# Preparation steps held on VectorE behind three more splits, and none ahead of a head's scores

## The chip, the cores and the metric

The kernel runs on one core of a Trainium2 chip. Its work goes through five engines, each with its own queue of instructions that it takes in order: TensorE (PE: matmuls and transposes), VectorE (DVE) and ScalarE (ACT) for elementwise work, GpSimd (POOL) and SyncE (SP), of which SP only starts transfers here and POOL starts some as well. An engine whose next instruction waits for something waits with everything behind it.

The metric is the device time of one launch in microseconds (us). Three runs of the kernel before gave 1018.87, 1021.4 and 1025.79 us, a median of 1021.4 us.

## The reference, cut to what matters

Two layers on `x` of 512 tokens by 1024 features, each `x = x + Mixer(RMSNorm(x))`: first gated linear attention (GLA), then a state-space mixer (S5), then a last RMSNorm. All is float32.

```python
# GLA: 4 heads, key size 128, value size 512; q, k, v, z, r are slices of h @ w_in
log_a = log_sigmoid(r @ w_gate_up + b_gate) / 16
b     = cumsum(log_a) within a chunk
att   = causal_mask((q * exp(b)) @ (k * exp(-b)).T)     # "scores"
o     = att @ v + (q * exp(b)) @ state_before_the_chunk  # state is carried from chunk to chunk
out   = (rms(o) * head_gain * silu(z)) @ w_out

# S5: 128 groups of 16 channels, 64 complex states each; u, z = split(h @ w_in)
lam_bar = exp(lam * dt);  b_bar = (lam_bar - 1) / lam * B
s_t   = lam_bar * s_(t-1) + b_bar @ u_t
y     = gelu(Re(C @ s) + d * u);  y = y * sigmoid(y @ w_glu + b_glu) * silu(z)
out   = y @ w_out
```

What S5 needs of powers of `lam_bar`, of `b_bar` and of `C` does not depend on `x`. The kernel builds these tables on the chip while the GLA layer runs. That is the "preparation" of the title.

## The kernel before, in words

**Arithmetic.** A float32 product is made of three matmuls on operands that are split in a high and a low part (`three`, L187 to L195): high by high, high by low, low by high. So every operand has to be split first: `split` (L155 to L162) writes the high part with ScalarE and the low part, source minus high, with VectorE; `split1` (L164 to L168) does both on VectorE.

**Weights.** They come in tiles of 128 x 1024 (512 KB), one load on SP's queue each (`wunit`, L173 to L184). Most are split by L158 (ScalarE) and L159 (VectorE). For `w_z`, `w_qk` and `w_v` of heads 1 to 3 (`dma=True`) the low part is made by a ScalarE copy and a GpSimd transfer that adds the source to it, so VectorE isn't needed there.

**The GLA layer** takes about the first 490 us, the S5 layer the rest. A head `h` of 1 to 3 goes so. The gate of the head (L422 to L446). The projections of q and k (`proj_qk`; VectorE takes them out of the PSUM banks at L460 and L461 and splits q at L159). Between these the output of the head before is transposed (`turn`: L399 on TensorE, L402 and a split on VectorE). Then the "weave", in which three things follow one another, one weight tile at a time: the projection of v (4 tiles), the product of the previous head's output with `w_out` (2 to 4 tiles), and the projection of z (4 tiles). Between the tiles the head's own attention is set in by a table of positions: `scores` (L484 a matmul, L486 a transpose of k, L488 the masked copy by VectorE, then splits), `state` (L502 to L506, splits at L170 and L171) and `mix`. The v tiles end in four PSUM banks `pd`, which VectorE and ScalarE empty at L161 and L162; the next tiles need these banks. The z tiles end in the same banks, emptied at L387 and L389, and the `w_out` tiles at L532.

**The preparation.** A plan of 43 steps lies ready: 17 F steps (tables from loaded constants, L1283 to L1301, and L1313; stores L1307 to L1309; then four loads for the next F step, among them `lpt` L1267, `s_bi` L1269 and `s_xc` L1272), 16 Z steps (L1323 on TensorE, L1327 on ScalarE, L1329 to L1333 on VectorE, a copy on SP that is called `gmd` here), 8 E steps (48 VectorE instructions on 128 x 512, L1251 to L1256, and transfers) and 2 G steps. A function `hook` is called once for each weight tile of the weave, and adds a rate to a counter; each time the counter passes one, a step is taken off the plan:

```python
pace[0] += RATES[phase[0]]      # phase is h - 1 for head h
while pace[0] >= 1: ...
    prep.step(mark, *st)
```

For heads 1 to 3, `hook` is also called `QZ[0]` times ahead of the head's weave, that is ahead of its scores. A head has 12 tiles in its weave, so before 14 calls of `hook`, at a rate of 0.84 or 0.88.

**What sets the order.** Tile, the layer that the kernel is written in, puts each engine's instructions in one fixed order when it builds the kernel. It may move instructions that do not depend on each other. A step of the preparation is held by `issue_after(mark[k])` for each of "pe", "act", "dve" and "sp": on each of these engines it may not stand ahead of the instruction last noted in `mark`. `mark["pe"]` is the last matmul of a `three`, `mark["sp"]` the last weight load, `mark["act"]` the last split of a weight tile on ScalarE; `mark["dve"]` is noted in `wunit` alone, and there only for the tiles that VectorE splits.

A part of the preparation that comes before the plan, called "small" (L985 to L1226), runs during head 0.

Of the kernel before, what the change touches and what calls it, by code (L numbers as in the profile page):

```python
# [19 lines left out]
MUL, ADD, SUB = ALU.mult, ALU.add, ALU.subtract  # L20

P = 128
# [37 lines left out]
USP = 50  # L60
SEQ0 = 'h0 u h2 u h4 u s h6 u x0 t x1 q0 q1 t'
GP = 4
RATES = [0.84, 0.84, 0.88, 0.94, 0.94]
LOWS = {'F': 30, 'Z': 30, 'E': 100, 'G': 0}
ETABS = [2, 3, 3, 3, 3, 3, 3, 3, 4, 4, 4, 4, 4, 4, 4, 7, 8]
POS = [[0, 0, 1, 2, 1, 2, 3, 1, 2, 3, 3], [0, 1, 1, 3, 4, 5, 6, 5, 5, 7, 9], [0, 1, 3, 4, 4, 5, 6, 5, 6, 8, 8], [1,
# [9 lines left out]
TORD = ['c0 c1 s0 c2 x0 s1 x1 c3 s2 x2 x3', 'c0 c1 c2 c3 x0 s0 s1 x1 s2 x2 x3', 'c0 c1 c2 c3 s0 x0 s1 s2 x1 x2 x3',  # L76
    'c0 c1 c2 c3 s0 s1 x0 x1 s2 x2 x3']
PACE = [2, 2, 2, 2, 2, 2, 3, 1, 2, 2, 2, 2, 2, 2, 2, 2, 2, 2, 1, 1, 1, 1]
QZ = [2, 3]
GPOS = [0, 0, 7]  # L80


def f(t):
    return t.bitcast(F32) if t.dtype == F32R else t
# [3 lines left out]
def trunk_kernel(  # L88
# [6 lines left out]
    V, A, G, S, PE = nc.vector, nc.scalar, nc.gpsimd, nc.sync, nc.tensor  # L95
# [58 lines left out]
    mark = {}  # L154
# [10 lines left out]
    def split1(dst_hi, dst_lo, src, scale=None):  # L165
        if scale is None:
            V.tensor_copy(out=dst_hi, in_=src)
            V.tensor_tensor(out=dst_lo, in0=src, in1=f(dst_hi), op=SUB)  # L168
        else:
            V.tensor_scalar(out=dst_hi, in0=src, scalar1=scale, scalar2=None, op0=MUL)  # L170
            V.scalar_tensor_tensor(out=dst_lo, in0=src, scalar=scale, in1=f(dst_hi), op0=MUL, op1=SUB)  # L171

    def wunit(src, nk, ncol, dma=False):  # L173
        raw = T_([P, nk, ncol], "wraw", WR)
# [150 lines left out]
    sm = prep.small(lam_re, lam_im, log_dt, s_d)  # L325
# [34 lines left out]
    def hook():  # L360
        pace[0] += RATES[phase[0]]
        while pace[0] >= 1:
# [29 lines left out]
    def turn(box, out_):  # L392
        oh, ol = out_

        def fn(tb):
            o2 = box[0][tb]
            pt = PT()
            for k in range(4):
                PE.transpose(pt[:, k * P:(k + 1) * P], o2[:, k * P:(k + 1) * P], ident)  # L399
            oh.append(q2(F32R))  # L400
            ol.append(q2(F32R))
            V.tensor_tensor(out=o2.rearrange("p (k c) -> p k c", k=4), in0=pt.rearrange("p (k c) -> p k c", k=4),  # L402
                            in1=hgp.unsqueeze(2).to_broadcast([P, 4, P]), op=MUL)
            split(oh[tb], ol[tb], o2)
        return fn

    rT = g4[:16, 1]
# [41 lines left out]
    def proj_qk(h, eq, ek):  # L449
        aq, ak = PO(), PO()  # L450
        for u in range(2):
            hi, lo = wunit(w_qk[h, u], 4, 256, dma=True)
            for m, acc in enumerate((aq, ak)):
                for k in range(4):
                    kb = 4 * u + k
                    three(acc, hi[:, k, m * P:(m + 1) * P], lo[:, k, m * P:(m + 1) * P],
                          hh[kb], hl[kb], kb == 0, kb == 7, True)
        q = eq
        k_ = ek
        V.scalar_tensor_tensor(out=q, in0=aq, scalar=float(P) ** -0.5, in1=eq, op0=MUL, op1=MUL)  # L460
        V.tensor_tensor(out=k_, in0=ak, in1=ek, op=MUL)  # L461
        qh = big(F32R)
        ql = big(F32R)
        split(qh, ql, q)
        return q, k_, qh, ql

    att_bufs = []
# [5 lines left out]
    class Attn:  # L473
# [6 lines left out]
        def scores(self, b):  # L480
            q, k_, qh, ql = self.qk
            cs = slice(b * P, (b + 1) * P)
            pa = PT()
            PE.matmul(pa[:, :P], lhsT=k_[:, cs], rhs=q[:, cs], start=True, stop=True)  # L484
            if b < NT - 1:
                PE.transpose(pa[:, P:2 * P], k_[:, cs], ident)  # L486
            at = att_bufs[b % 2]
            V.copy_predicated(out=at, mask=cmask, data=pa[:, :P])  # L488
            sm = self.sm[b] = big(F32R)
            if b < NT - 1:  # L490
                split(sm[:, 2 * P:3 * P], sm[:, 3 * P:], pa[:, P:2 * P])
            split1(sm[:, 0:P], sm[:, P:2 * P], at)

        def state(self, b):
            es, sm = self.es, self.sm[b]
# [922 lines left out]
```

## Time and profile before

| | |
|---|---|
| median of three runs | 1021.4 us |
| lowest and highest | 1018.87 and 1025.79 us |
| the profiled execution's own time | 1022.88 us |
| its span in the trace | 1021.1 us |
| mean granted TensorE clock | 0.946 of full speed |
| PE busy | 922.1 us, 90% of the span |
| VectorE busy | 716.5 us, 70% |
| ScalarE busy | 461.3 us, 45% |
| GpSimd busy | 138.3 us, 14% |

The trace is of one execution. A row of a timeline has the start, the duration, the engine, the line of the kernel, the operation, output and inputs by the program's names, their shape, and in brackets the time that the engine sat idle before it and what released it. An instruction's duration includes its latency; the next one of the same engine starts earlier than its end, so what a row of instructions takes is read from the distance of their starts. The granted clock of TensorE is given as a share of the full one: 1.00 is the higher of its two levels, 0.5 the lower.

### The profile page before, as it was taken

How to read it: one execution, taken by the hardware profiler on the slowest of the kernel's cores; microseconds unless marked ns; L12 is line 12 of the kernel's file. 1: busy time of each engine (PE TensorE's matmuls, PEld its weight loads, DVE VectorE, ACT ScalarE, POOL GpSimd, SP SyncE). 2: the span in 40 equal slices, each digit the busy share in tenths (PEclk: the TensorE clock that was granted, in tenths of full speed). 3: DMA queues.
4: the chain of work that ended last, by engine and by line, in shares of the span. 5: the costliest groups of instructions: out<-in, count | busy, mean ns of one | idle time of the engine just before them, and what ended most of it. 6: DMA issues, size and time to landing. Idle time of an engine off the chain costs nothing.

```text
span 1021.1 us, 13513 instructions
## 1 busy us (share of the span) xinstructions
PE 922.1 (90%) x5019; PEld 720.5 (71%) x5019; DVE 716.5 (70%) x1186; ACT 461.3 (45%) x660; POOL 138.3 (14%) x238
## 2 busy tenths in 40 slices
PE   6798936998499987969998799999899999999996
PEld 5576735776367765757777688778687888888885
DVE  5795699897998797899447759798997541424422
ACT  5554533456346543434366653843624432323312
POOL 4151822231011411112110000000000000000000
PEclk9998977999699997979999899999899999999999
DMA  8887667999769998998862638578854423262213
GB/s 263 229 189 163 156 175 205 314 322 272 236 194 272 299 298 233 275 336 255 248 200 101 203 126 272 189 267 271 257 174 140 142 84 103 89 178 100 86 62 82
DMA packets 114801, 205.81 MB, mean 202 GB/s; under 512 B 30080, under 2 KB 65456, under 8 KB 114736
## 3 DMA queue, kind: packets, MB, share of 16 engines
q1 hardware_dynamic: 98544, 153.81, 48.1%
q0 software_dynamic: 13376, 46.16, 17.7%
q10 hardware_dynamic: 2816, 4.99, 1.5%
q8 instruction: 39, 0.64, 0.2%
q14 instruction: 26, 0.21, 0.1%
HBM read 167.69 MB, written 45.62 MB: 209 GB/s over the span
## 4 chain that ended last, share of the span: by engine, by line
PE 54%; DMA 19%; DVE 12%; ACT 5%; issue 5%; POOL 2%; SPq 2%; POOLq 0%; ACTq 0%; DVEq 0%
PE pd L193 7%; PE pd L194 6%; PE pd L195 6%; DMA q<-s_bi 6%; PE pd L190 6%; PE pd L189 6%; PE pd L191 6%; DMA wraw<-w_v 2%; ACT u L725 2%; PE po L189 1%; PE po L190 1%; PE pt L189 1%; PE pt L190 1%; PE po L191 1%; PE pt L191 1%
## 5 line engine op out<-in xcount | busy, mean ns | idle before, releaser
L159 DVE TENSOR_TENSOR whl<-wraw,whl 128x1024 fp32r<-128x1024 f32 x100 | 122.4, 1225 | 162.4 <-ACT whl L158 152.3
L158 ACT CAST whl<-wraw 128x1024 fp32r<-128x1024 f32 x100 | 104.9, 1050 | 212.3 <-PE pd L194 64.3
L193 PE MATMUL pd<-whl,actA 128*128 128x512 f32 x384 | 153.9, 406 | 12.7 <-ACT whl L158 8.9
L195 PE MATMUL pd<-whl,actA 128*128 128x512 f32 x384 | 153.9, 402 | 0.0
L194 PE MATMUL pd<-whl,actA 128*128 128x512 f32 x384 | 153.8, 400 | 0.0
L189 PE MATMUL pd<-actA,whl 128*128 128x512 f32 x256 | 102.9, 410 | 9.5 <-ACT u L725 7.5
L191 PE MATMUL pd<-actA,whl 128*128 128x512 f32 x256 | 102.6, 401 | 0.0
L193 PEld LDWEIGHTS pd<-whl,actA 128*128 128x128 f32 x384 | 73.8, 193 | 30.9 <-ACT whl L158 8.9
L193 PE MATMUL pd<-whl,q 128*128 128x512 f32 x192 | 80.6, 421 | 15.9 <-DVE big L162 8.5
L195 PEld LDWEIGHTS pd<-whl,actA 128*128 128x128 f32 x384 | 73.6, 192 | 16.6 <-issue 1.2
L194 PEld LDWEIGHTS pd<-whl,actA 128*128 128x128 f32 x384 | 73.8, 192 | 16.2 <-issue 0.8
L194 PE MATMUL pd<-whl,q 128*128 128x512 f32 x192 | 78.8, 411 | 0.0
L180 ACT CAST whl<-wraw 128x1024 fp32r<-128x1024 f32 x36 | 37.7, 1048 | 72.0 <-PE pd L194 31.0
L189 PEld LDWEIGHTS pd<-actA,whl 128*128 128x128 f32 x256 | 49.3, 193 | 22.8 <-ACT u L725 9.1
L193 PEld LDWEIGHTS pd<-whl,q 128*128 128x128 f32 x192 | 38.1, 199 | 28.1 <-DVE big L162 10.3
L191 PEld LDWEIGHTS pd<-actA,whl 128*128 128x128 f32 x256 | 49.1, 192 | 11.4
L189 PE MATMUL po<-actA,whl 128*128 128x512 f32 x128 | 52.4, 410 | 4.2 <-ACT whl L180 4.2
L195 PE MATMUL pd<-whl,q 128*128 128x512 f32 x128 | 53.2, 418 | 0.0
L191 PE MATMUL po<-actA,whl 128*128 128x512 f32 x128 | 50.9, 400 | 1.2 <-DMA whl<-w_qk 1.2
L190 PE MATMUL pd<-actA,whl 128*128 128x512 f32 x128 | 51.8, 405 | 0.0
L725 ACT ACTIVATE u<-pd,rsP 64x256 f32<-64x256 f32 x64 | 48.0, 749 | 3.2 <-DVE mxr L718 2.3
L190 PE MATMUL pd<-big,whl 128*128 128x512 f32 x120 | 48.2, 403 | 0.0
(333 smaller groups left out, 2025.9 us busy)
## 6 DMA issues: line engine op xcount, KB each, us to landing
wraw<-w_glu SPq DMA_DIRECT2D x32, 512.0 KB, 3.4
wraw<-w_v SPq DMA_DIRECT2D x16, 512.0 KB, 6.4
wraw<-w_z SPq DMA_DIRECT2D x16, 512.0 KB, 8.1
whl<-w_z POOLq DMA_DIRECT2D x16, 512.0 KB, 8.5
wraw<-w_out SPq DMA_DIRECT2D x16, 512.0 KB, 6.7
q<-lpt SPq DMA_DIRECT2D x16, 512.0 KB, 8.6
q<-s_bi SPq DMA_DIRECT2D x16, 512.0 KB, 9.4
tab<-q POOLq DMA_DIRECT2D x32, 256.0 KB, 7.6
```

What stands on the lines that cost most here:

```text
L158: i0 = A.copy(out=dst_hi, in_=src)
L159: i1 = V.tensor_tensor(out=dst_lo, in0=src, in1=f(dst_hi), op=SUB)
L180: A.copy(out=hi, in_=raw)
L189: PE.matmul(acc, lhsT=wh, rhs=ah, start=first, stop=False)
L190: PE.matmul(acc, lhsT=wh, rhs=al, start=False, stop=False)
L191: mark["pe"] = PE.matmul(acc, lhsT=wl, rhs=ah, start=False, stop=last).ins
L193: PE.matmul(acc, lhsT=ah, rhs=wh, start=first, stop=False)
L194: PE.matmul(acc, lhsT=ah, rhs=wl, start=False, stop=False)
L195: mark["pe"] = PE.matmul(acc, lhsT=al, rhs=wh, start=False, stop=last).ins
L725: A.activation(out=dst, in_=src, func=AF.Copy, scale=rsP[hs, tb:tb + 1])
```

## The change

Three things. `RATES` for the three heads goes from 0.84, 0.84, 0.88 to 1.0, 1.0, 1.05. `QZ[0]` goes from 2 to 0: no call of `hook` ahead of a head's weave. So a head has 12 calls at 1.0 or 1.05 instead of 14 at 0.84 or 0.88 (12.0, 12.0 and 12.6 steps instead of 11.8, 11.8 and 12.3). And `mark["dve"]` is now also noted at the last VectorE instruction of three splits: of the transposed output in `turn`, of q in `proj_qk`, and of the scores. A step that is taken off the plan after one of these may not stand ahead of it on VectorE.

```diff
--- before.py
+++ after.py
@@ -60,7 +60,7 @@
 USP = 50
 SEQ0 = 'h0 u h2 u h4 u s h6 u x0 t x1 q0 q1 t'
 GP = 4
-RATES = [0.84, 0.84, 0.88, 0.94, 0.94]
+RATES = [1.0, 1.0, 1.05, 0.94, 0.94]
 LOWS = {'F': 30, 'Z': 30, 'E': 100, 'G': 0}
 ETABS = [2, 3, 3, 3, 3, 3, 3, 3, 4, 4, 4, 4, 4, 4, 4, 7, 8]
 POS = [[0, 0, 1, 2, 1, 2, 3, 1, 2, 3, 3], [0, 1, 1, 3, 4, 5, 6, 5, 5, 7, 9], [0, 1, 3, 4, 4, 5, 6, 5, 6, 8, 8], [1,
@@ -76,7 +76,7 @@
 TORD = ['c0 c1 s0 c2 x0 s1 x1 c3 s2 x2 x3', 'c0 c1 c2 c3 x0 s0 s1 x1 s2 x2 x3', 'c0 c1 c2 c3 s0 x0 s1 s2 x1 x2 x3',
     'c0 c1 c2 c3 s0 s1 x0 x1 s2 x2 x3']
 PACE = [2, 2, 2, 2, 2, 2, 3, 1, 2, 2, 2, 2, 2, 2, 2, 2, 2, 2, 1, 1, 1, 1]
-QZ = [2, 3]
+QZ = [0, 3]
 GPOS = [0, 0, 7]
 
 
@@ -165,10 +165,11 @@
     def split1(dst_hi, dst_lo, src, scale=None):
         if scale is None:
             V.tensor_copy(out=dst_hi, in_=src)
-            V.tensor_tensor(out=dst_lo, in0=src, in1=f(dst_hi), op=SUB)
+            i1 = V.tensor_tensor(out=dst_lo, in0=src, in1=f(dst_hi), op=SUB)
         else:
             V.tensor_scalar(out=dst_hi, in0=src, scalar1=scale, scalar2=None, op0=MUL)
-            V.scalar_tensor_tensor(out=dst_lo, in0=src, scalar=scale, in1=f(dst_hi), op0=MUL, op1=SUB)
+            i1 = V.scalar_tensor_tensor(out=dst_lo, in0=src, scalar=scale, in1=f(dst_hi), op0=MUL, op1=SUB)
+        return i1.ins
 
     def wunit(src, nk, ncol, dma=False):
         raw = T_([P, nk, ncol], "wraw", WR)
@@ -401,7 +402,7 @@
             ol.append(q2(F32R))
             V.tensor_tensor(out=o2.rearrange("p (k c) -> p k c", k=4), in0=pt.rearrange("p (k c) -> p k c", k=4),
                             in1=hgp.unsqueeze(2).to_broadcast([P, 4, P]), op=MUL)
-            split(oh[tb], ol[tb], o2)
+            mark["dve"] = split(oh[tb], ol[tb], o2)[1]
         return fn
 
     rT = g4[:16, 1]
@@ -461,7 +462,7 @@
         V.tensor_tensor(out=k_, in0=ak, in1=ek, op=MUL)
         qh = big(F32R)
         ql = big(F32R)
-        split(qh, ql, q)
+        mark["dve"] = split(qh, ql, q)[1]
         return q, k_, qh, ql
 
     att_bufs = []
@@ -489,7 +490,7 @@
             sm = self.sm[b] = big(F32R)
             if b < NT - 1:
                 split(sm[:, 2 * P:3 * P], sm[:, 3 * P:], pa[:, P:2 * P])
-            split1(sm[:, 0:P], sm[:, P:2 * P], at)
+            mark["dve"] = split1(sm[:, 0:P], sm[:, P:2 * P], at)
 
         def state(self, b):
             es, sm = self.es, self.sm[b]
```

From line 169 on, the changed kernel's line numbers are one higher than before.

The order of VectorE's queue at three places shows what moved. The numbers in the names are buffers. First, VectorE at the start of head 1, from the first emptying of q and k's banks on (L460, L461 after). `big_1045` is q, `big_1046` is k, L402 is the transposed output of head 0, `whl` are weight tiles, and lines from L1250 on are the preparation. Before:

```order
L460 SCALAR_TENSOR_TENSOR big_1045<-po_1071,big_1045 128x512
L159 TENSOR_TENSOR q_202_1147<-big_868,q_201_1146 128x512
L461 TENSOR_TENSOR big_1046<-po_1072,big_1046 128x512
L402 TENSOR_TENSOR big_879<-pt_1151,hgp 128x512
L1284 TENSOR_TENSOR q_206_1161<-q_207_1162 128x8x64
L1292 TENSOR_TENSOR q_208_1168<-big_1018,pp_1019 128x1024
L1251 TENSOR_TENSOR q_233_1237<-big_933,big_935 128x512
L1254 TENSOR_TENSOR q_233_1237<-big_933,big_936 128x512
L1251 TENSOR_TENSOR q_242_1298<-big_933,big_935 128x512
L1254 TENSOR_TENSOR q_242_1298<-big_933,big_936 128x512
L159 TENSOR_TENSOR whl_1559<-wraw_1556,whl_1558 128x1024
L159 TENSOR_TENSOR big_1138<-big_1045,big_1137 128x512
```

After:

```order
L461 SCALAR_TENSOR_TENSOR big_1045<-po_1071,big_1045 128x512
L159 TENSOR_TENSOR whl_1478<-wraw_1475,whl_1477 128x1024
L462 TENSOR_TENSOR big_1046<-po_1072,big_1046 128x512
L159 TENSOR_TENSOR q_202_1147<-big_868,q_201_1146 128x512
L159 TENSOR_TENSOR big_1138<-big_1045,big_1137 128x512
L403 TENSOR_TENSOR big_879<-pt_1151,hgp 128x512
L159 TENSOR_TENSOR whl_1559<-wraw_1556,whl_1558 128x1024
L159 TENSOR_TENSOR q_205_1157<-big_879,q_204_1156 128x512
L489 COPY_PREDICATED att_122<-cmask,pt_1205 128x128
L167 CAST big_1209<-att_122 128x128
L168 TENSOR_TENSOR big_1209<-att_122,big_1209 128x128
L159 TENSOR_TENSOR big_1209<-pt_1205,big_1209 128x128
```

Six preparation instructions stood between k (L461) and the split of q (`big_1138`) and none stands there now; the masked copy of the first scores (L489 after) comes at once.

Second, VectorE at the four emptyings of v's banks in head 3 (L162 with `rstd`). L1283 is the instruction of an F step that reads the loaded `s_bi`, L488 and L168 are the scores. Before, the first and the second of them:

```order
L162 SCALAR_TENSOR_TENSOR big_3039<-pd_3043,rstd_73_457,big_3035 128x512
L168 TENSOR_TENSOR big_3150<-att_124,big_3150 128x128
L1299 TENSOR_TENSOR bh_3093<-big_3010,BA 128x128
L1308 TENSOR_TENSOR q_693_3330<-q_644_3090,q_693_3330 128x1024
L1294 TENSOR_TENSOR q_670_3241<-big_3100,pp_3101 128x1024
L1283 TENSOR_TENSOR q_707_3396<-q_674_3255,q_675_3256 128x1024
L488 COPY_PREDICATED att_122<-cmask,pt_3305 128x128
L1301 TENSOR_TENSOR bh_3093<-bh_3093,bh_646_3094 128x128
L162 SCALAR_TENSOR_TENSOR big_3040<-pd_3044,rstd_73_457,big_3036 128x512
L1329 SCALAR_TENSOR_TENSOR tmp_3164<-pt_3159,par,tmp_3164 128x128
L1313 TENSOR_TENSOR q_671_3247<-q_671_3247,q_670_3241 128x1024
```

After, all four:

```order
L162 SCALAR_TENSOR_TENSOR big_3021<-pd_3025,rstd_73_457,big_3017 128x512
L1300 TENSOR_TENSOR bh_3142<-big_2884,BA 128x128
L162 SCALAR_TENSOR_TENSOR big_3022<-pd_3026,rstd_73_457,big_3018 128x512
L1330 SCALAR_TENSOR_TENSOR tmp_3195<-pt_3190,par,tmp_3195 128x128
L162 SCALAR_TENSOR_TENSOR big_3023<-pd_3027,rstd_73_457,big_3019 128x512
L1285 TENSOR_TENSOR q_649_3132<-q_650_3133 128x8x64
L1293 TENSOR_TENSOR q_651_3139<-big_2884,pp_2885 128x1024
L162 SCALAR_TENSOR_TENSOR big_3024<-pd_3028,rstd_73_457,big_3020 128x512
```

Between the first and the second emptying stood five preparation instructions, among them L1283; now one small one stands there.

Third, VectorE at the first emptyings of z's banks in head 3 (L387, after L388; L526 and L389 belong to the same stage). This is the last head, and the `w_out` tiles and the S5 layer come behind it. Before:

```order
L387 SCALAR_TENSOR_TENSOR tmp_3692<-tmp_3692,pd_3422 128x512
L1287 TENSOR_TENSOR q_769_3677<-q_770_3678 128x8x64
L1332 CAST kf_3510<-tmp_3508 128x128
L1308 TENSOR_TENSOR q_800_3812<-q_746_3560,q_800_3812 128x1024
L1301 TENSOR_TENSOR bh_3563<-bh_3563,bh_748_3564 128x128
L387 SCALAR_TENSOR_TENSOR tmp_3696<-tmp_3696,pd_3423 128x512
L526 TENSOR_TENSOR rsv_3618<-rsv_3618,rstd_73_457 128x4
L1330 SCALAR_TENSOR_TENSOR tmp_3632<-dm,kd,tmp_3632 128x16
L1294 TENSOR_TENSOR q_770_3678<-big_3570,pp_3571 128x1024
L1333 TENSOR_TENSOR kf_3510<-tmp_3508,kf_3510 128x128
L1300 TENSOR_TENSOR bh_773_3688<-big_3570,BB 128x128
```

After:

```order
L388 SCALAR_TENSOR_TENSOR tmp_3692<-tmp_3692,pd_3422 128x512
L1286 TENSOR_TENSOR q_745_3554<-q_711_3410,q_712_3411 128x8x64
L1287 TENSOR_TENSOR q_745_3554<-q_711_3410,q_712_3411 128x8x64
L388 SCALAR_TENSOR_TENSOR tmp_3696<-tmp_3696,pd_3423 128x512
L1333 CAST kf_3510<-tmp_3508 128x128
L1302 TENSOR_TENSOR bh_3563<-bh_3563,bh_748_3564 128x128
L1331 SCALAR_TENSOR_TENSOR tmp_3632<-dm,kd,tmp_3632 128x16
L527 TENSOR_TENSOR rsv_3618<-rsv_3618,rstd_73_457 128x4
L1288 TENSOR_TENSOR q_744_3553<-q_745_3554 128x8x64
L1309 TENSOR_TENSOR q_761_3623<-q_708_3402,q_761_3623 128x1024
L1334 TENSOR_TENSOR kf_3510<-tmp_3508,kf_3510 128x128
L1301 TENSOR_TENSOR bh_773_3688<-big_3570,BB 128x128
```

The preparation instructions here are of earlier steps of the plan after the change than before: what was ahead of this place is now partly at it and behind it.

## Rows read from the trace of the kernel before

**Rows 1.** Windows: stretch, length, busy time per engine, granted clock, DMA share, GB/s.

```profile
130.00:490.00 360.00, 301.88 (x1319) 228.28 (x1318) 319.02 (x534) 167.57 (x247) 70.54 (x104) 0.90 0.89 263
490.00:1021.00 531.00, 507.54 (x3227) 405.41 (x3225) 308.52 (x433) 224.91 (x310) 10.30 (x30) 0.98 0.50 160
134.00:166.00 32.00, 8.61 (x30) 5.46 (x30) 31.23 (x56) 8.67 (x14) 4.96 (x9) 0.58 0.63 181
166.00:219.00 53.00, 53.00 (x229) 40.52 (x228) 48.16 (x77) 29.16 (x41) 14.15 (x20) 1.00 0.95 294
262.00:286.00 24.00, 9.68 (x39) 5.64 (x38) 22.05 (x45) 7.63 (x13) 2.68 (x5) 0.57 0.82 252
...
446.00:510.00 64.00, 62.56 (x300) 49.76 (x299) 50.14 (x83) 27.15 (x46) 10.99 (x21) 0.95 0.84 263
```

**Rows 2.** Timeline of PE: matmuls that ended a long idle time.

```profile
151.95 0.80 PE L484 MATMUL pt<-big,big 128*128 128x128 f32 x2 [11.19 <-DVE big L159]
...
159.31 1.08 PE L1323 MATMUL pt<-q,bh 128*32 128x256 f32 x8 [5.92 <-DVE att L488]
...
269.57 0.80 PE L484 MATMUL pt<-big,big 128*128 128x128 f32 x2 [6.42 <-DVE tmp L1329]
...
394.64 0.79 PE L193 MATMUL pd<-whl,q 128*128 128x512 f32 x1 [5.04 <-DVE big L162]
...
444.17 0.80 PE L193 MATMUL pd<-whl,q 128*128 128x512 f32 x1 [7.46 <-DVE tmp L387]
```

**Rows 3.** Timeline of DVE: preparation instructions of two sizes, back to back.

```profile
141.25 0.68 DVE L1251 TENSOR_TENSOR q<-big,big 128x512 f32<-128x512 f32 x1
141.85 0.69 DVE L1254 TENSOR_TENSOR q<-big,big 128x512 f32<-128x512 f32 x1
...
173.53 1.22 DVE L1308 TENSOR_TENSOR q<-q,q 128x1024 f16<-128x1024 f32 x1
174.67 1.22 DVE L1313 TENSOR_TENSOR q<-q,q 128x1024 f32<-128x1024 f32 x1
```

**Rows 4.** Timeline of DVE: first and second emptying of v's banks, head 3.

```profile
382.99 0.75 DVE L162 SCALAR_TENSOR_TENSOR big<-pd,rstd,big 128x512 fp32r<-128x512 f32 x1
...
392.30 1.23 DVE L1283 TENSOR_TENSOR q<-q,q 128x1024 f32<-128x1024 f32 x1 [5.89 <-DMA q<-s_bi]
...
393.64 0.29 DVE L1301 TENSOR_TENSOR bh<-bh,bh 128x128 f32<-128x128 f32 x1
393.84 0.75 DVE L162 SCALAR_TENSOR_TENSOR big<-pd,rstd,big 128x512 fp32r<-128x512 f32 x1
```

**Rows 5.** Timeline of DVE: first emptying of z, head 3, and S5's start.

```profile
443.43 0.68 DVE L387 SCALAR_TENSOR_TENSOR tmp<-tmp,pd 128x512 f32<-128x512 f32 x1
...
509.88 0.69 DVE L718 TENSOR_REDUCE mxr<-pd 128x4 f32<-128x512 f32 x1 [0.58 <-PE pd L195]
```

**Rows 6.** Timeline of DVE: two instructions of the small preparation in head 0.

```profile
80.43 0.28 DVE L1162 TENSOR_REDUCE tmp<-pt 64x2 f32<-64x128 f32 x1
...
82.97 0.21 DVE L1171 COPY tmp<-tmp 64x128 f32<-64x128 f32 x1
```

**Rows 7.** Lines by form: busy and mean ns, then idle time before by releaser.

```profile
L1283 DVE TENSOR_TENSOR q<-q,q 128x1024 f32<-128x1024 f32 x16 | 19.6, 1223 | 14.2 <-DMA q<-s_bi 12.2 <-issue 1.9
L1292 DVE TENSOR_TENSOR q<-big,pp 128x1024 f32<-128x1024 f32 x16 | 19.6, 1223 | 15.7 <-DMA big<-s_xc 9.7 <-DMA pp<-pw 5.6 <-DVE q L1284 0.3
```

**Rows 8.** Chain of waits: start, length, what: a load of head 2.

```profile
217.46 17.08 DMA wraw<-w_v
```

**Rows 9.** The page, part 6: issues, KB each, median us from issue to landing.

```profile
wraw<-w_v SPq DMA_DIRECT2D x16, 512.0 KB, 6.4
...
q<-lpt SPq DMA_DIRECT2D x16, 512.0 KB, 8.6
q<-s_bi SPq DMA_DIRECT2D x16, 512.0 KB, 9.4
...
big<-s_xc SPq DMA_DIRECT2D x16, 256.0 KB, 9.7
```

## The prediction

> **What bounds the kernel now.** I read the windows first, since the averages over the span hide two stages. From 490 us on TensorE is busy for 507.54 of 531 us at a granted clock of 0.98 [rows 1]: the S5 layer is bound by matmuls, and nothing in this change makes fewer of them. The GLA layer is different. From 130 to 490 us TensorE is busy for 301.88 of 360 us at a clock of 0.90, VectorE for 319.02 us, and the transfers hold a share of 0.89 [rows 1]. To VectorE's 319 us belong its waits for loads of the preparation, 14.2 us ahead of L1283 and 15.7 us ahead of L1292 [rows 7]: together 349 of 360 us, so its queue leaves next to nothing free. The windows at the heads' starts show who waits for whom: 134 to 166 us has 8.61 us of TensorE beside 31.23 us of VectorE, 262 to 286 us has 9.68 beside 22.05 [rows 1]. The timeline of TensorE names the releaser, each time an instruction of VectorE: 11.19, 5.92, 6.42, 5.04 and 7.46 us are the five largest of these waits, 36.0 us together [rows 2]. The reader is to see that TensorE here waits not for the work it needs but for what stands ahead of it on VectorE. That is what the change moves.
>
> **How I price a moved instruction.** From the distance of two starts: a preparation instruction on 128x1024 takes 1.14 us of the queue, one on 512 elements 0.60 us [rows 3], one on 128 elements 0.20 us [rows 4]. I counted the preparation instructions of each size that stand on VectorE's queue ahead of an anchor, in the order before and in the order after, and multiplied. Ahead of the first emptying of v's banks (L162) of head 1 stand 7, 19 and 4 of the three sizes before (20.2 us), 3, 11 and 3 after (10.6 us): 9.6 us less. For head 2 it is 88.6 against 71.6 us, for head 3 143.6 against 130.8 us. Ahead of the first emptying of z's banks (L387) of head 3 it is 177.3 against 164.5 us. All 43 steps are still done, so what is missing there stands later.
>
> **A, the queue ahead of head 3's z: -12.8 us.** A term may be taken once along a queue: head 2 inherits head 1's gain, so I take the last anchor at which the queue is still the bound, the first L387 of head 3, and not the sum over heads. TensorE waits there for 7.46 us [rows 2]. The bound from above is 12.8 us, if VectorE's queue is the limit all the way, which 349 of 360 us says; from below 0, if loads then set the pace. I take 12.8, because the five waits of 36.0 us give three times that room, and all end in VectorE's instructions.
>
> **B, the tail: +2.5 us.** What was taken away ahead comes back behind the first L387 of head 3. Between the first and the fourth of these emptyings stand 3.9 us of preparation before and 7.4 us after: 3.5 us that TensorE may have to wait for the last bank. Over the whole stretch from that L387 to the first L718 of S5 I count 51.7 us of VectorE's work before and 66.9 us after, 15.2 us more, and the stretch lasts from 443.43 to 509.88 us, 66.5 us [rows 5]. Its cover is TensorE: from 446 to 510 us it is busy for 62.56 of 64 us, VectorE for 50.14, so 13.9 us are free [rows 1]. 15.2 us against 13.9 leaves 1.3 us over, and 2.5 us is the middle between that and the 3.5 us at the z banks. The ends are 0 and 15.2 us, all of it uncovered. By the first L718 the queue holds 2.4 us more than before, by the fourth the same, so nothing is handed on to S5.
>
> **C, head 0: +2 us.** Two transposes of the small preparation (L1160 and L1173) stood some 30 matmuls apart on TensorE's queue and stand side by side after. Between them lies a chain on VectorE from L1162 at 80.43 to L1171 at 82.97 us with 0.21 us for itself: 2.75 us [rows 6], with TensorE behind it and no cover. The ends are 0, if the chain has run by then, and 2.75; I take 2, nearer to the row.
>
> **D, the wait for s_bi in head 3: -4 us.** Between the first and second L162 of head 3 stood L1283, which waited for its load for 5.89 us [rows 4], and TensorE's matmul behind the second L162 waited 5.04 us [rows 2]. One instruction of 0.20 us stands there now. TensorE's matmuls need the bank that this L162 empties, and now get it without that load. The ends are 5.04 us gained and 0, if the load delays VectorE all the same a little later and ahead of the z banks. I take 4, since the next emptyings follow without an F step between, and the wait then falls where TensorE has matmuls of `w_out` in stock.
>
> **Counted at nothing.** The rates: 36.6 steps fall due in the heads instead of 35.8, less than one step, and behind the last head the tail holds it. The fixed hold itself issues no instruction. On SP's queue two `w_v` loads of head 2 now stand ahead of a `gmd` copy; one such load took 17.08 us [rows 8] against a median of 6.4 [rows 9]. That may give up to the 10.7 us between these, hidden unless VectorE's queue ceases to be the bound; its own row is in the third rival.
>
> **The sum.** -12.8 + 2.5 + 2 - 4 = -12.3 us. It is made against the profiled execution of 1022.88 us, 1.5 us above the median of 1021.4: 1022.9 - 12.3 = 1010.6, rounded **1010.5 us**. With the ends of B, C and D the forecast case reaches from 1002 (all at their good ends 1022.9 - 12.8 - 5.0 = 1005.1, and 3 us for the waits at the lower clock level, at which the head starts run with 0.58 and 0.57 [rows 1]) to 1014.6 (D at nothing).
>
> **Rival 1, transfers set the pace (1014 to 1024, about 1019.5).** Taking the steps out of the head starts puts them into the weave, and the weave of head 1, from 166 to 219 us, already has a transfer share of 0.95 at 294 GB/s and VectorE busy for 48.16 of 53 us [rows 1]. An F step loads 512 KB twice and 256 KB [rows 9], 1.31 MB, which at 294 GB/s is 4.5 us. If one F step each of heads 1 and 2 lands that much later, 9 us of the 12.3 are given back: 1019.6. For it: L1283 and L1292 already wait 29.9 us for loads [rows 7]. Against it: the early loads have more time when VectorE comes to the steps later. The Trainium skill's page "DMA: Bandwidth & Descriptors" (Queues, rings and completion order) says that each transfer engine takes its queue rows in turn, packet by packet; by that rule preparation loads and weight tiles would slow one another in the weave in whichever order they were issued, and the sum would be the 1019.6 us above. The 17.08 us of one load agrees with that, and doesn't show its cause.
>
> **Rival 2, slower (about 1038).** The place is the tail behind the first L387 of head 3. The price is B at its far end, 15.2 us of preparation in front of the splits of `w_out` and of S5's first weights (L159), on a VectorE whose 13.9 free us lie in pieces where it waits for others, not where work is ready. It decides if the head starts give nothing back because the loads end there, A and D at 0: 1022.9 + 15.2 = 1038.1. From about 9 us of uncovered tail with no gain ahead it would count as slower. For it: a window with 62.56 of 64 us of TensorE busy has no room for anything late. Against it: each of the five waits ahead ends at VectorE, and none at a load directly.
>
> **Rival 3, more than the sum (about 1000).** If the preparation no longer stands in front of anything that TensorE waits for at a head's start, its idle time goes, not the queue's length alone. In the two windows at heads 1 and 2 TensorE is idle for 23.4 + 14.3 = 37.7 us [rows 1], and with the 7.46 us of head 3 that is 45.2. Half of it is 22.6: 1000.3. The order speaks for it (six instructions between L461 and the split of q, none after); VectorE's 349 of 360 us speak against it, since the steps put back must still be done in the same time.
>
> **Chances.** What this kernel's measurement can tell from no change is about 1%: below 1011.2 is faster, above 1031.6 slower. The forecast has 0.48, of which three quarters lie below 1011.2; rival 1 has 0.23, rival 2 has 0.16, rival 3 has 0.13. Faster: 0.36 + 0.13 = 0.49. Same: 0.12 + 0.23 + 0.01 of rival 2 = 0.36. Slower: 0.15. The range from 999 to 1024 us takes in the forecast, rival 1 and more than half of rival 3, about 0.8; rival 2 lies outside.
>
> **What would show it.** In the changed kernel's profile the wait of 11.19 us ahead of the first scores of head 1 should shrink by more than half, and the first L387 of head 3 should come about 13 to 17 us earlier on the trace (A and D). From there to the first L718 should take 67 to 70 us (B). Head 1's start should be up to 2 us later than 130 us (C). Were the weaves of heads 1 and 2 longer than 53 us with waits for `s_bi` and `s_xc` above the 29.9 us, rival 1 is what happened; were L387 early and L718 not, rival 2. I would be wrong altogether if L387 of head 3 came at 443 us again: then VectorE's queue was not the bound of the GLA layer.

## The result

| | changed | before |
|---|---|---|
| median, 17 runs each | 1025.49 us | 1019.57 us |
| lowest to highest | 1022.59 to 1033.54 us | 1014.57 to 1025.79 us |
| profiled execution, its span | 1024.55, 1022.8 us | 1022.88, 1021.1 us |

Ratio 1.0055, 95% interval 1.0036 to 1.0074: the change costs some 5.6 us, where 10.9 us were forecast to be gained (1010.5 against the median of 1021.4 us then known). It is within the 1% named as "same", but clear of no change and on the other side. The two traces are 1.7 us apart in span: the profiled execution of before lies 3.3 us above its median, that of the changed kernel 0.9 us below. So the traces show where time moved, but some 4 us of the loss lie in the spread between executions.

### The profile page after: what moved, and what is told of

It reads as the page before. It is cut to its first block, busy times and chain, and to the rows that moved or that the text cites. A ratio compares the mean times of both kernels' runs of the same rounds, so it can differ in the third digit from the quotient of the medians.

```text
span 1022.8 us, 13500 instructions
## 1 busy us (share of the span) xinstructions
PE 920.8 (90%) x5019; PEld 719.3 (70%) x5019; DVE 716.9 (70%) x1186; ACT 461.0 (45%) x660; POOL 137.9 (13%) x238
## 4 chain that ended last, share of the span: by engine, by line
PE 54%; issue 16%; DVE 11%; DMA 8%; ACT 7%; POOL 4%; SPq 0%; POOLq 0%; ACTq 0%; DVEq 0%
PE pd L194 6%; PE pd L196 6%; PE pd L195 6%; PE pd L191 5%; PE pd L190 5%; PE pd L192 5%; ACT u L726 4%; PE po L190 3%; PE po L192 3%; PE po L191 3%; DMA q<-s_bi 2%; DMA bmd<-q 2%; PE pt L191 1%; PE pt L190 1%; PE pt L192 1%
## 5 line engine op out<-in xcount | busy, mean ns | idle before, releaser
L194 PE MATMUL pd<-whl,actA 128*128 128x512 f32 x384 | 153.8, 406 | 13.9 <-ACT whl L158 8.9
L194 PE MATMUL pd<-whl,q 128*128 128x512 f32 x192 | 81.9, 428 | 12.2 <-DVE big L162 5.9
L195 PE MATMUL pd<-whl,q 128*128 128x512 f32 x192 | 79.9, 416 | 0.0
L1308 ACT CAST q<-q 128x1024 f16<-128x1024 f32 x32 | 33.2, 1042 | 69.4 <-DMA bmd<-q 36.2
L181 ACT CAST whl<-wraw 128x1024 fp32r<-128x1024 f32 x36 | 37.7, 1048 | 52.9 <-PE pd L195 17.5
L192 PEld LDWEIGHTS pd<-actA,whl 128*128 128x128 f32 x256 | 48.7, 190 | 11.2
L196 PE MATMUL pd<-whl,q 128*128 128x512 f32 x128 | 54.0, 427 | 0.0
```

The source lines that it names most:

```text
L181: A.copy(out=hi, in_=raw)
L192: mark["pe"] = PE.matmul(acc, lhsT=wl, rhs=ah, start=False, stop=last).ins
L194: PE.matmul(acc, lhsT=ah, rhs=wh, start=first, stop=False)
L195: PE.matmul(acc, lhsT=ah, rhs=wl, start=False, stop=False)
L196: mark["pe"] = PE.matmul(acc, lhsT=al, rhs=wh, start=False, stop=last).ins
L1308: nc.scalar.copy(out=hl[:, 0], in_=src)
```

## The profile after

The same windows as [rows 1], with the same columns; the last is the weave of head 3, from the last emptying of v to the last of z. Before, that weave takes 52.5 us, from 398.48 to 450.98:

```profile
130.00:490.00 360.00, 299.87 (x1301) 226.04 (x1299) 312.01 (x526) 162.30 (x231) 64.41 (x95) 0.90 0.86 257
134.00:166.00 32.00, 20.39 (x77) 14.00 (x76) 30.68 (x57) 9.54 (x14) 5.79 (x10) 0.79 0.53 157
446.00:510.00 64.00, 57.86 (x251) 45.02 (x252) 56.88 (x90) 25.71 (x44) 13.79 (x29) 0.89 0.82 269
383.11:447.59 64.48, 51.96 (x224) 39.18 (x224) 56.26 (x94) 26.49 (x39) 8.77 (x14) 0.87 0.94 286
```

At head 1's start TensorE has 20.39 us of work where it had 8.61: that part came as forecast. From 446 to 510 us it has 57.86 where it had 62.56, at a granted clock of 0.89 instead of 0.95: a part of the time goes there. The timeline of TensorE shows the waits that answer to [rows 2]:

```profile
89.91 0.43 PE L1174 MATMUL pt<-ident,tmp 64*128 64x64 f32 x2 [3.35 <-DVE tmp L1172]
...
140.72 0.58 PE L485 MATMUL pt<-big,big 128*128 128x128 f32 x1 [4.75 <-DVE big L159]
...
256.99 0.80 PE L485 MATMUL pt<-big,big 128*128 128x128 f32 x2 [5.64 <-DVE big L159]
...
335.06 0.80 PE L190 MATMUL po<-actA,whl 128*128 128x512 f32 x1 [9.52 <-ACT big L521]
...
431.05 1.08 PE L1324 MATMUL pt<-q,bh 128*32 128x256 f32 x8 [4.07 <-DVE q L1314]
...
435.10 0.79 PE L194 MATMUL pd<-whl,q 128*128 128x512 f32 x1 [2.97 <-DVE tmp L388]
...
447.13 0.80 PE L194 MATMUL pd<-whl,q 128*128 128x512 f32 x1 [3.29 <-DVE xx L533]
...
466.55 0.42 PE L290 MATMUL pt<-ident,xx 128*128 128x128 f32 x1 [2.02 <-DVE xx L533]
```

Head 1's wait of 11.19 us is 4.75 now. In its place stand waits inside the weaves (335, 431, 435 us) and in the tail (447, 466 us). All of TensorE's idle time before its instructions from 130 to 515 us is 59.6 us before and 60.7 us after. The row at 89.91 us, in head 0, belongs to term C.

The largest wait, 9.52 us in the weave of head 2, begins with a load:

```profile
328.18 1.23 DVE L1293 TENSOR_TENSOR q<-big,pp 128x1024 f32<-128x1024 f32 x1 [4.87 <-DMA pp<-pw]
...
330.93 1.05 ACT L1308 CAST q<-q 128x1024 f16<-128x1024 f32 x1 [3.66 <-DVE q L1287]
```

VectorE waits 4.87 us for `pp` and then does the preparation; ScalarE waits for that with the cast L1308, which stands in its queue ahead of L521, and TensorE waits for L521. In weave 2 of the kernel before TensorE has 0.3 us of idle time in all. With small loads (e5) or less preparation (e9) this wait is not in the trace; with `pp` loaded first (e16) it is 7.22 us.

VectorE just ahead of the wait at 435 us shows what makes that one:

```profile
424.95 0.75 DVE L171 SCALAR_TENSOR_TENSOR big<-big,ges,big 128x512 fp32r<-128x512 f32 x1
...
425.82 1.22 DVE L1295 TENSOR_TENSOR q<-big,pp 128x1024 f32<-128x1024 f32 x1
426.95 1.22 DVE L1284 TENSOR_TENSOR q<-q,q 128x1024 f32<-128x1024 f32 x1
...
428.35 1.21 DVE L1309 TENSOR_TENSOR q<-q,q 128x1024 f16<-128x1024 f32 x1
...
429.69 1.22 DVE L1314 TENSOR_TENSOR q<-q,q 128x1024 f32<-128x1024 f32 x1
...
431.96 0.68 DVE L1285 TENSOR_TENSOR q<-q 128x512 f32<-128x512 f32 x1
432.56 1.22 DVE L1293 TENSOR_TENSOR q<-big,pp 128x1024 f32<-128x1024 f32 x1
...
434.38 0.67 DVE L388 SCALAR_TENSOR_TENSOR tmp<-tmp,pd 128x512 f32<-128x512 f32 x1
```

Between the head's own split (L171) and the first emptying of z lie 9.4 us of queue, 7.6 of them preparation. The milestones of VectorE that answer to [rows 4, 5]:

```profile
383.11 0.74 DVE L162 SCALAR_TENSOR_TENSOR big<-pd,rstd,big 128x512 fp32r<-128x512 f32 x1
...
511.63 0.68 DVE L719 TENSOR_REDUCE mxr<-pd 128x4 f32<-128x512 f32 x1
```

The last v of head 3 comes at 383.11 instead of 398.48 us, 15.4 us early; the first z at 434.38 instead of 443.43, 9.0 early; the last z at 447.59 instead of 450.98, 3.4 early; S5 starts 1.75 us late, and takes 511.2 us in both traces.

These are single traces, and their milestones scatter. Two kernels of the experiments, e3 (change) and e4 (before), have within 2.2 us of preparation the same work as these two ahead of the first z of head 3. In their traces the last v comes at 389.08 against 401.04 us, 12.0 early, the first z at 441.36 against 443.38, 2.0 early, and S5 starts 4.1 us late. So single places are sure to some 6 or 7 us only; that the gain is there at v and gone by S5 is in both pairs.

The next table cuts VectorE's timeline at these milestones. "Start" is from the first emptying of q (L460) to the last of v, "weave" from there to the next head's q (head 3: to its last z), "tail" from there to the first L718. Each cell has the length and in brackets the preparation in it (by distances of starts, at most the duration), in us. The slope is that of length over preparation across the traces of all 20 kernels told of here, and r its correlation.

| | before | changed | slope | r |
|---|---|---|---|---|
| start 1 | 28.3 (17.7) | 23.0 (11.2) | 0.76 | 0.82 |
| weave 1 | 92.3 (52.1) | 90.0 (48.9) | 0.78 | 0.59 |
| start 2 | 30.2 (19.7) | 31.0 (15.9) | 0.93 | 0.76 |
| weave 2 | 68.9 (37.7) | 73.8 (45.5) | 0.77 | 0.69 |
| start 3 | 41.7 (20.8) | 36.8 (12.5) | 0.85 | 0.83 |
| weave 3 | 52.5 (31.3) | 64.5 (38.9) | 1.12 | 0.93 |
| tail | 58.9 (15.5) | 64.0 (27.2) | 0.44 | 0.72 |

Up to head 1's q another 8.7 us are gained. By these slopes a microsecond of preparation costs about as much in a weave as at a head's start; they are a correlation over kernels that differ in other things too. The starts lost 18.6 us of it and got 9.4 us shorter; weaves 2 and 3 got 15.4 us more and are 16.9 us longer; the tail got 11.7 us more and is 5.1 us longer.

## The experiments

Each ratio is to the kernel before, timed beside it, with its 95% interval. Where two kernels are compared in us, it is by their ratios.

**The parts of the change.** e1: the three notes of `mark["dve"]` alone.

```diff
-RATES = [1.0, 1.0, 1.05, 0.94, 0.94]   -QZ = [0, 3]
+RATES = [0.84, 0.84, 0.88, 0.94, 0.94] +QZ = [2, 3]
```

> The change's three notes of mark["dve"] alone: RATES and QZ as before. Ahead of the first emptying of z in head 3 stand 165.9 us of preparation on VectorE (177.3 before, 164.5 with the whole change), so 33.1 us are left behind it (21.7 before, 34.5 with the change). Theory, the tail: what is pushed behind head 3's z is not covered there, so this is as slow as the whole change, 1023 to 1027 us. Rival, the denser weave: the loads of steps crowded into the weave by the higher rates set the pace; without the rates it is as before, 1018 to 1021 us.

1038.79 us, 1.0171 (1.0135 to 1.0207): slower than both theories said. With `QZ[0]` at 2 the notes put two hooks' steps exactly behind the split of q and ahead of the scores: start 3 is 45.6 us. Its trace starts S5 7.0 us later than before's. Its S5 layer is 8.5 us longer too, with a wait for a stored table that is half of that; what makes the rest is not shown:

```profile
743.09 0.21 PE L766 MATMUL pt<-q,q 128*128 128x64 f16 x1 [4.28 <-DMA q<-bmd]
```

e2: `RATES` and `QZ` alone, without the notes.

> RATES and QZ of the change alone, no new notes of mark["dve"]. Ahead of the first z of head 3 stand 173.7 us of preparation, 25.3 us are left behind it, 3.6 us more than before. Theory, the tail: 1019 to 1022 us, near the kernel before. Rival, the denser weave: as slow as the whole change, 1023 to 1027 us, since all steps are in the weave here too.

1024.07 us, 1.0021 (0.9989 to 1.0052): no measurable difference, as the tail theory had it, but its interval overlaps that of the change. e8: the change without the notes at the scores and in `turn`.

```diff
-            mark["dve"] = split(oh[tb], ol[tb], o2)[1]
+            split(oh[tb], ol[tb], o2)
-            mark["dve"] = split1(sm[:, 0:P], sm[:, P:2 * P], at)
+            split1(sm[:, 0:P], sm[:, P:2 * P], at)
```

> RATES and QZ of the change and the note at the split of q alone, none at the scores and at the transposed output. Ahead of the first z of head 3 stand 175.1 us of preparation, ahead of the v of heads 1, 2, 3 17.8, 76.4 and 143.1 us. Theory, the tail (time follows what is left behind that z): 1019 to 1023 us. Theory, loads (time follows the steps in the weave): 1023 to 1027 us.

1021.12 us, 1.0007 (0.9985 to 1.0029), again as the tail theory had it, and clear of the change. Together: neither part is good alone; the two notes that e8 lacks are what costs, and notes without the new rates and `QZ` cost most.

**The tail.** e3, the change, and e4, the kernel before, with VectorE's work of the last steps left out:

```diff
+        if ck < 4:    # E: u products, difference, sum
+        if cb < 14:   # F: z2 and z + z2
+        if cb < 15:   # F: two of four products of bo
```

> The whole change, with 15.3 us of VectorE's preparation left out, nearly all of it behind the first z of head 3 (four of six products and sums of the last four E steps, the second product and its sum of the last two F steps, two products of the last F step; all loads, stores and other work stay, the tables come out incomplete). 19.2 us are left behind that z. Theory, the tail: the 10.7 us that the stretch from the first z of head 3 to S5 is longer in the changed kernel's trace come back, 1012 to 1017 us. Rival, loads and weight tiles set the pace of that stretch: nothing of that, 1022 to 1026 us.

> The kernel before with the same VectorE work left out as in e3 (2.2 us of it ahead of the first z of head 3, 13.1 us behind). Theory, the tail: there the tail was covered, so little is gained, 1016 to 1020 us, and e3 is then the faster of the two by 2 to 6 us. Rival, loads set the pace: 1018 to 1021 us, and e3 stays slower than this by about 6 us.

e3 1025.66 us, 1.0012 (0.9985 to 1.0040); e4 1019.48 us, 0.9983 (0.9962 to 1.0004). By the ratios e3 gains 0.43% on the change, some 4.4 us for 15.3 us of work, and e4 1.7 us. The 2.7 us between them are less than the intervals allow to tell from nothing: the tail is at most a part of the loss, and not the 8 to 13 us that I expected of it.

**The loads.** e5, the change, and e6, the kernel before, with an eighth of lpt, s_bi and s_xc:

```diff
-        S.dma_start(out=lp, ... [1, n]]))
+        S.dma_start(out=lp[:, :2 * NS], ... [1, 2 * NS]]))   # bb and xc alike
+        lp4, bb4 = (t[:, 0:1].to_broadcast([P, GB, 2, NS]) for t in (lp4, bb4))
```

> The whole change, with the preparation's loads of lpt, s_bi and s_xc cut to an eighth (1.31 MB to 0.16 MB per F step; the computations read the loaded eighth eight times, so the tables are wrong; VectorE's instructions keep their sizes, and ahead of each head's anchors stand within 2.2 us of the same preparation as with the change). Theory, loads: the head starts' gain is given back in the weaves because F steps wait there for loads, and weight tiles share the transfers with them; without these bytes this kernel is 1003 to 1012 us, and faster than e6 by 3 us or more. Rival, the tail and the queue order alone: both kernels gain alike, 1015 to 1022 us, and this one stays some 6 us behind e6.

> The kernel before with the same three loads cut to an eighth. Its waits ahead of L1283 and L1292 (29.9 us, of which 21.9 for s_bi and s_xc) go, but TensorE's waits at the head starts are for what stands ahead on VectorE's queue and stay. Theory, loads: 1008 to 1016 us, slower than e5. Rival: 1010 to 1018 us, faster than e5.

e5 1017.15 us, 0.9947 (0.9922 to 0.9972); e6 1006.79 us, 0.9869 (0.9840 to 0.9898). Smaller loads gain both kernels some 11 to 13 us, and the change stays about 8 us behind. So the loads are not what ate the gain. The two traces show where it goes: with small loads the change is 4.6 us ahead at the last v of head 3, 3.5 us behind at the first z and 8.0 us behind at the last z, and S5 starts 8.7 us late. Weave 3 has 40.5 against 31.4 us of preparation and takes 65.3 against 52.7 us. e14 (change) and e15 (before) with the loads of a step written first, e16 with pp ahead of lpt:

```diff
+                if cb + 1 < NB: self.load(cb + 1)
                 if cb < NB: self.compute(cb)
-                if cb + 1 < NB: self.load(cb + 1)
```

> The change with the four loads of an F step written ahead of its computation instead of behind. VectorE's order is nearly the same (within 3.3 us at every anchor). Theory, in the weaves VectorE's work and not the loads is what costs: within 3 us of the change, 1022 to 1028 us. Rival, late loads: the 22.4 us of waits ahead of L1284 and L1293 shrink, 1012 to 1020 us.

> The kernel before with the loads of an F step written first. There leaving out VectorE's work gave nothing (e10) and small loads gave 13 us (e6), so if earlier issue helps the loads at all, it helps here: 1010 to 1017 us. If the loads are bound by the transfers' rate or by free buffers and not by their issue: 1018 to 1025 us.

> The change with the small load pp issued ahead of the three large ones of its F step instead of behind; VectorE's order is the same at every anchor. VectorE waits 13.0 us for pp in the changed kernel. Theory, the weave is bound by VectorE's work: the waits move to s_xc or vanish, and 0 to 6 us are gained, 1019 to 1026 us. Rival, these waits are what the change costs: 1012 to 1016 us.

e14 1032.33 us, 1.0115 (1.0077 to 1.0153); e15 1023.25 us, 1.0020 (0.9991 to 1.0048); e16 1030.18 us, 1.0090 (1.0055 to 1.0125). None gains. VectorE's waits changed their place: in e16 those for pp fell from 13.0 to 6.3 us and those for s_bi rose from 9.4 to 15.2. Why e14 and e16 are slower than the change is open.

**The weave.** e7, the change with more steps in the weaves of heads 1 and 2, and so fewer left for the tail:

```diff
-RATES = [1.0, 1.0, 1.05, 0.94, 0.94]
+RATES = [1.15, 1.15, 1.05, 0.94, 0.94]
```

> The change with RATES 1.15, 1.15, 1.05: the notes and QZ stay. Ahead of the first z of head 3 stand 189.4 us of preparation on VectorE (177.3 before, 164.5 with the change), so only 9.6 us are left behind it; ahead of the v of heads 1, 2 and 3 stand 10.6, 77.8 and 144.4 us (20.2, 88.6, 143.6 before). Theory, the tail: with the tail empty it is faster than the change by 4 us or more, 1015 to 1021 us. Theory, loads: the weaves are denser still, so it is no faster than the change, 1024 to 1032 us.

1044.23 us, 1.0225 (1.0198 to 1.0253): the emptied tail doesn't help, and it is slower than the loads theory had it too. Weaves 1, 2 and 3 have 57.6, 51.1 and 45.1 us of preparation and take 101.3, 84.5 and 70.0 us. TensorE's two longest waits of weave 3:

```profile
440.57 0.80 PE L194 MATMUL po<-big,big 128*128 128x512 f32 x1 [5.57 <-ACT big L521]
...
466.70 0.79 PE L194 MATMUL pd<-whl,q 128*128 128x512 f32 x1 [9.84 <-DVE tmp L388]
```

That made me drop tail and loads, and test the weave itself. e9, the change, and e10, the kernel before, without the second product and its sum in eight F steps:

```diff
+    SKIP = (6, 7, 8, 9, 11, 12, 13, 14)
+        if cb not in self.SKIP:   # z2 = x4 * pp, and z = z + z2
```

> The whole change, with the second product and its sum left out of F steps 6 to 9 and 11 to 14 (two VectorE instructions on 128 x 1024 each, 18.2 us in all; 6.9 us of it in the weave of head 2, 7.9 us in that of head 3, behind the last emptying of v; loads, stores and matmuls stay, the tables come out wrong). Theory, the weave: there the preparation is not hidden, since VectorE does it ahead of the weave's own instructions and TensorE waits for those, so the weaves of heads 2 and 3 get shorter by about what is left out, 10 us or more: 1008 to 1016 us. Rival, the weave is covered by matmuls and only loads or the tail count: 1020 to 1025 us.

> The kernel before with the same instructions left out: 3.2 us of the weave of head 2, 4.8 us of that of head 3, 10 us at the heads' starts and elsewhere. Theory, the weave: VectorE's work costs about the same at a head's start as in a weave, so this gains as much as e9 does against the change: 1002 to 1011 us. Rival: only what stood at the heads' starts is gained, 5 to 8 us, 1012 to 1016 us, and then the change, with the starts already clear, gains less than this kernel does.

e9 1008.71 us, 0.9871 (0.9832 to 0.9910); e10 1023.68 us, 1.0008 (0.9982 to 1.0034). The 18.2 us left out give the change 1.8%, about 18.8 us, and the kernel before nothing. Weave 3 of e9 against 64.48 us above:

```profile
384.11:437.15 53.04, 48.23 (x206) 35.78 (x205) 48.76 (x88) 24.14 (x36) 9.09 (x14) 0.94 1.06 333
```

7.9 us less preparation go with 11.4 us less time, at a clock of 0.94 instead of 0.87; in weave 2 it is 6.7 and 2.8 us. In e10 weaves 2 and 3 have 3.0 and 4.8 us less preparation than before and are 4.9 and 2.1 us longer: the slopes of the table are no price that holds everywhere. VectorE waits there for loads, 34.2 us against 29.9 in [rows 7], the longest one at head 2's end:

```profile
350.11 1.23 DVE L1283 TENSOR_TENSOR q<-q,q 128x1024 f32<-128x1024 f32 x1 [9.66 <-DMA q<-s_bi]
```

Its trace starts S5 6.5 us early and loses 5.1 us in S5, so part of e10's answer lies outside the GLA layer. S5 takes from 506.6 to 519.7 us in the 20 traces, and what makes that is not settled. e13, the change with fewer steps in the weaves of heads 2 and 3, nothing left out:

```diff
-RATES = [1.0, 1.0, 1.05, 0.94, 0.94]
+RATES = [1.0, 0.85, 0.85, 0.94, 0.94]
```

> The change with RATES 1.0, 0.85, 0.85: the notes and QZ stay, some 5 steps fewer are taken in the weaves of heads 2 and 3 and done behind the last z. Preparation on VectorE in the weave of head 3 falls to 33.0 us in the order (38.9 with the change, 31.1 before), behind the first z of head 3 stand 48.2 us (34.5 with the change). Theory, the weave costs about 1 us per us and the tail about 0.3 (e9 and e3): -6 to -7 in the weaves, +3 to +4 in the tail, 1019 to 1024 us, faster than the change by 2 to 5. Rival, what is left behind that z decides: 1029 to 1036 us.

1023.19 us, 1.0024 (1.0000 to 1.0049), 3.1 us better than the change by the ratios, as expected, though the two intervals overlap. Weave 3 falls to 55.2 us (33.0 of preparation), the tail grows to 73.0 us (39.6), and the S5 layer takes 8.2 us longer behind it.

**VectorE's work on GpSimd.** e11 (before) and e12 (change): the sum; e17 (change) and e18 (before): the three small instructions of an F step.

```diff
-        self.nc.vector.tensor_tensor(out=z, in0=z, in1=z2, op=ADD)
+        self.nc.gpsimd.tensor_tensor(out=z, in0=z, in1=z2, op=ADD)   # e11, e12
-        tt(out=bh, ...); tt(out=b2, ...); tt(out=bh, ...)
+        gt(out=bh, ...); gt(out=b2, ...); gt(out=bh, ...)            # e17, e18; gt on GpSimd
```

> The kernel before with the sum of an F step (L1313, 16 of 128 x 1024, 18.2 us of VectorE) on GpSimd. Nothing is left out. On GpSimd a sum of 128 x 256 takes 0.82 us, so one of these takes some 3.3 us and 52 us in all, ahead of the transfers that GpSimd issues for weight tiles. If VectorE's work in the GLA layer costs about one to one: 1004 to 1014 us. If GpSimd's transfers come late for it, or the two engines hinder one another: 1020 to 1035 us.

> The whole change with the sum of an F step on GpSimd, as in e11. If VectorE's work costs one to one in the weave: 1008 to 1018 us, and it stays some 5 us behind e11. If GpSimd's transfers come late for it: 1025 to 1040 us.

> The change with the three 128 x 128 instructions of an F step (L1300 to L1302, 48 in all, 9.6 us of VectorE) on GpSimd, where one takes 0.5 to 0.6 us; nothing is left out. Ahead of the last z of head 3 stand 162.7 us of preparation on VectorE (171.9 with the change). If VectorE's preparation costs 0.7 to 1.1 us per us ahead of that z, as the traces of the runs so far say: 1015 to 1020 us, 6 to 9 us less than the change. If GpSimd's late transfers cost more than that, as in e12: 1026 to 1035 us.

> The kernel before with the same three instructions on GpSimd: 172.0 us ahead of the last z of head 3 (181.2 before). By the same prices 1011 to 1015 us, faster than both; if in the kernel before VectorE's work is not what bounds (e10), 1018 to 1022 us; if GpSimd's transfers come late, 1023 to 1030 us.

e11 1020.78 us, 0.9993 (0.9964 to 1.0022); e12 1043.76 us, 1.0231 (1.0182 to 1.0280); e17 1028.38 us, 1.0066 (1.0042 to 1.0090); e18 1016.93 us, 0.9954 (0.9927 to 0.9981). e11 gains nothing, and e12 is 18 us slower than the change, as their rivals said. e18 beats the kernel before by 4.7 us, the low end of what was expected; e17 gains nothing, which is what its rival said. So the price per microsecond cannot be used alone. What GpSimd takes over stands ahead of the transfers that it issues; that this is the reason was not tested. The sum in e11:

```profile
L1313 POOL TENSOR_TENSOR q<-q,q 128x1024 f32<-128x1024 f32 x16 | 56.6, 3535 | 82.6 <-DVE q L1294 58.1 <-DMA q<-lpt 12.6 <-DVE tmp L1330 11.2
```

## Why the prediction was wrong

**What bounds (half right).** That TensorE waits at the starts for what stands ahead on VectorE was right, and the change clears it. But e6 gains 13 us from smaller loads and e10 nothing from less VectorE work, so "349 of 360 us" counted VectorE's waits for loads as if they were its work: in the kernel before they grow when work is taken out, from 29.9 to 34.2 us in e10. VectorE's work is not free there either, since e18 gains 4.7 us from 9.6 us of it moved.

**A and D (right at the starts, gone by z).** Between the sum of -12.3 us and the 1.75 us by which the trace starts S5 late lie 14 us: up to the first z of head 3 (A, C and D) 14.8 us were forecast and 9.0 are there, and behind it (B) 10.8 us are lost instead of 2.5. A and D together asked for 16.8 us at the first z of head 3. 15.4 us were there at the last v of head 3, 51 us earlier, and 9.0 at that z. D was right where it was put: the four emptyings of v in head 3 take from 378.9 to 383.1 us, where they took from 383.0 to 398.5. The step that failed is the choice of anchor: "the first L387 of head 3" was taken as the place up to which less preparation ahead means less time. Between v and z of head 3 the table's slope is 1.12 us of time per us of preparation, and e9 and the pair e5 and e6 show that weave paying. The preparation was put where I had written of "TensorE matmuls in stock"; the stock ended, as the wait of 4.07 us for a preparation matmul's own input and the 2.97 us for L388 show. That matmul (L1324) is in TensorE's queue, in order, which I had not priced. Nor had I priced that a load of the preparation reaches TensorE by way of VectorE and ScalarE, as in the wait of 9.52 us.

**B (the term that was mis-sized).** From the first L387 to the first L718 I forecast 2.5 us more; it is 77.25 against 66.45 us, 10.8 more. I set VectorE's 15.2 us against its 13.9 free us and took the rest. The extra preparation stood ahead of the emptyings L388 and L533, which TensorE waits for (2.97 and 3.29 us), and the clock granted from 446 to 510 us fell from 0.95 to 0.89. I had named 15.2 us as the far end of B, but the reach of the forecast, 1002 to 1014.6 us, left it out. But with 15.3 us taken out (e3) only 4.4 us come back, so the tail's preparation is not all of this.

**C (the mechanism right, its price open).** The wait is there: in the changed kernel TensorE waits 3.35 us ahead of the second transpose (89.91 us), where it waited for nothing before. The first z of head 0 comes at 103.1 us all the same, against 103.2. Over all traces it comes at 102.8 to 105.9 us in the eleven kernels with the transposes side by side, and at 100.4 to 103.5 in eight of the nine with them apart (107.5 in e6). So the equal times may be luck, and a cost up to the 2 us forecast is not excluded. By head 1's q 8.7 us are gained, where C asked for a later start. In this stretch VectorE lost the preparation ahead of q (among it L1283, after 1.03 us of idle time) and waits for other engines: 3.18 us for a table to be stored and 3.02 us for ScalarE's half of a weight split, which stands behind q now. A counted the work; these waits were in no term.

**The rivals.** Rival 1 (transfers) has one of its two signs: weave 2 is 4.9 us longer, but VectorE's waits for s_bi, s_xc and pp fall from 29.9 to 22.4 us, and with small loads the change is still behind (e5, e6). Its sentence on queue rows could not bear on the order of these loads: the preparation's and the weight tiles' stand on one queue, SP's [rows 9]. Rival 2 named the stretch behind the first z, which is 10.8 of its 15.2 us, but asked that the starts gain nothing; they did gain. Rival 3 counted the starts alone; at heads 1 and 2 TensorE's idle time in its windows did fall, from 23.4 to 11.6 and from 14.3 to 3.8 us, and came back later.

**What stays open.** That the weaves of the changed kernel pay for VectorE's preparation is shown (e9 against e10, and e5 against e6). Why the kernel before doesn't is open: it is shown only in total (e10), and its weaves then got longer with less preparation in them. What the wait of 9.52 us, which begins with a load, is worth by itself, why e17 gains nothing while e9 gains all of it, why moving loads costs the change, and the 4 us by which the medians differ more than the traces, are not settled.

## What to carry to other kernels

Work taken from in front of one stage stands in front of the next: price the place where it lands by what waits behind it there, not by the busy share of that stage. A stretch with TensorE 100% busy, as weave 2 was before, is no cover if its matmuls need the same queue that the moved work joins: 7.8 us of preparation more, and TensorE waits 9.52 us in one place there. And before a sum of queue time is called a bound, leave some of that work out of the kernel before: if nothing comes back, as in e10, the sum may have counted waits as work.

## What the runs showed of the hardware

A float32 sum of 128 x 1024 took 3.54 us on GpSimd (e11) against 1.22 us on VectorE, and the three instructions of 128 x 128 took 0.81 to 1.23 us (e18), where 0.5 to 0.7 us was read from other instructions of that size (L985).
